# Half-size feature block last, bank copies first, re-ordered loads and setup in a two-layer encoder kernel

## The chip, the cores and the metric

The kernel runs on one core of one Trainium2 chip, as one program. The metric is the device time in microseconds (us); each time is a median of several runs. A profile of one execution is read beside it: PE is TensorE's matmul row and PEld its weight loads, DVE is VectorE, ACT is ScalarE, POOL is GpSimd, SP is SyncE, which issues most of the loads.

## What is computed

Two encoder layers on x (512 tokens by 1024, float32). Each layer adds half of a SwiGLU feed-forward, then three attention mixers that run on the same normalised x, then half of a second feed-forward:

```python
for l in range(DEPTH):                      # 2
    x = x + 0.5 * swiglu(rms_norm(x, ffn1_norm[l]), ffn1_wg[l], ffn1_wu[l], ffn1_wd[l])
    h = rms_norm(x, mix_norm[l])
    ...                                     # h @ w_in[l], split; differential, dilated and latent attention
    x = x + mix @ w_o[l]
    x = x + 0.5 * swiglu(rms_norm(x, ffn2_norm[l]), ffn2_wg[l], ffn2_wu[l], ffn2_wd[l])
# swiglu(x, wg, wu, wd) = (silu(x @ wg) * (x @ wu)) @ wd, with 2816 features
```

## The kernel before

The program is a chain of stages: feed-forward, mixer, feed-forward, and the same again for the second layer. Four feed-forward stages (`ffn`, L249) hold most of the time. Every float32 product is split into a high and a low part in the fast float32r type and made of three matmuls (`mm3`); a weight tile `raw` is split by ScalarE into `whi` (L63) and by VectorE into `wlo` (L64).

**Blocks.** The 2816 features are 22 tiles of 128, worked through in blocks (`FF_BLOCKS`, L38): one block of 2 tiles, then five of 4. For each block an "up" product makes gate and up together, then a "down" product adds the block's share to x. The order is up(0), up(1), down(0), up(2), down(1) and so on; within an up product, after its first two groups, the previous block's result `hid` is transposed and turned into the operand of its down product (`hidden_operand`, L330).

**Seven products.** Both kinds are done by the class `Seven`: a 2 x 2 block product with seven multiplications in place of eight (a Strassen form). `fetch` (L187) loads five keys of weights, 11, u1, 21, u3 and 22, through SyncE; u1 and u3 are the sums of two weights, and the second addend is added by a DMA on GpSimd's queue (L193). For a block of 4 an up product has ten tiles of 512 KB, a down product five; a block of 2 has tiles of half the size. The tiles share ten slots (`N_RAW`). `run` (L225) issues the multiplications into the PSUM banks A, B and D, two banks (t = 0, 1) of each. Where one partial sum belongs to two results, `seed` (L201) copies it, negated, from one bank into another (ScalarE, L208), and TensorE goes on adding there. `done` reads a finished bank: in an up product ScalarE and VectorE write `hid` (L285 to L307), in a down product VectorE adds the bank to x (L316). In a down product the multiplication into A that follows the seed of A is the last one.

**Stage head.** A feed-forward stage transposes x on TensorE (L133), and ScalarE and VectorE make four operands with all their sums (L66, L67, L365 to L368, L168 to L173) in two buffers `c`. `token_factor` (L136) squares x on ScalarE (L141). The mixer (L469) begins in the same way: eight transposes, splits into `xg` (L482), then projections (`project`, L502), which walk the eight k tiles in order.

**Setup.** `setup` (L410) loads gains, bias table, lambdas and the rotary tables. It is emitted after the first feed-forward stage, its DMAs go on GpSimd's queue, and it borrows two weight slots (`oh`, `vec`). Ten `drep` writes broadcast the bias table to DRAM.

**What sets the order.** SyncE's queue is kept as written (`manual_schedule`). The instructions of the other engines are ordered by a planner before the run, by readiness and by the order in which they were emitted; on the chip each engine then works through its own list in order. Two engines that touch the same PSUM bank are put one after the other, in the order of emission, also when both only read.

Of the kernel before, what the change touches and what calls it, by code (L numbers as in the profile page):

```python
# [23 lines left out]
KD = D // P  # L24
# [12 lines left out]

FF_BLOCKS = (2, 4, 4, 4, 4, 4)  # L38


@with_exitstack
def encoder_kernel(ctx: ExitStack, tc, T: dict, out):
# [132 lines left out]
    class Seven:  # L175
# [10 lines left out]

        def fetch(self):  # L187

            for key, ij, plus in (("11", "11", 0), ("u1", "12", "11"), ("21", "21", 0), ("u3", "12", "22"), ("22", "22", 0)):
                for h in range(len(self.parts)):  # L190
                    t = self.raw[key, h] = wload(self.src(ij, h), [P, len(self.parts[h]), self.w])
                    if plus:
                        nc.gpsimd.dma_start(t, self.src(plus, h), accum_op=ALU.add)  # L193
# [31 lines left out]
        def run(self, done):  # L225

            for t, o in self.multiply(I_A11, "11", "A", True, False):
                done("q1", t, o)
                self.seed("B", t, o)
# [8 lines left out]
            self.add("21", "u1", "21")  # L238
            for t, o in self.multiply(I_S3, "u3", "B", False, True):
                done("w", t, o)  # L240
                self.seed("A", t, o)
            last = [lambda: self.multiply(I_S4, "22", "D", False, True), lambda: self.multiply(I_A22, "21", "A", False, True)]
# [5 lines left out]

    def ffn(l, pre, fp, last=False, first=False):  # L249
        def tmp(shape=(P, 512)):  # L250
# [93 lines left out]
        blocks, m0 = [], 0  # L344
# [4 lines left out]

        xa = [operand() for _ in range(4)]  # L350
        if first:
            load_x(0)
        ups = [gate_up(*b) for b in blocks]
        if first:
            ups[0].fetch()
            load_x(1)
        for k in range(4):
            h, lo = xa[k]
# [19 lines left out]

        def run_up(i, between):
            if not (first and i == 0):  # L380
                ups[i].fetch()
            hids[i] = fp.tile([P, NT, 512], F32, tag="c8", bufs=2, name=nm("hid"))
            w = blocks[i][1] * P
            for _ in ups[i].run(gate_up_done(w, hids[i])):
                between()
# [83 lines left out]
    def mixer(l, sb):  # L469
# [11 lines left out]

        xg = []  # L482
        for k in range(KD):
            px = x_transposed(k, "ABCDABDE"[k])
            hl = tuple(t2k("xg", N_XG, F32R) for _ in range(2))
            split(*hl, px, gcol("mix_norm", l, k))
            xg.append(hl)
        r = token_factor(lambda: t2k("a", N_A))
# [13 lines left out]
        def project(c0, n, put, tags="AA"):  # L502

            wl_ = []

            def load():
                cs = c0 if isinstance(c0, tuple) else (c0,)
                w = n // len(cs)
                most = 4 if n <= 256 else 3
                for a in range(0, KD, most):  # L510
                    m = min(most, KD - a)
                    raw = wraw([P, m, n])
                    for i, c in enumerate(cs):
                        nc.sync.dma_start(raw[:, :, i * w:(i + 1) * w], win[:, a:a + m, c:c + w])
                    h, lo = wsplit(raw, [P, m, n])
                    wl_.extend((h[:, k, :], lo[:, k, :]) for k in range(m))

            def piece(t):
                if t == 0:
                    load()  # L520
                pp = bank(tags[t % 2])
                tk = slice(t * P, (t + 1) * P)
                mm3(pp[:, :n], [(a[:, tk], b[:, tk]) for a, b in xg], wl_)
                put(t, pp[:, :n], r[:, t:t + 1])
# [225 lines left out]
        ups = {}  # L750
# [286 lines left out]
    for l in range(L):  # L1037
        with tc.tile_pool(name=f"f{l}", bufs=1, reuse_waits="tile") as fp:
            ffn(l, "ffn1", fp, first=(l == 0))
            if l == 0:  # L1040
                setup()
        with tc.tile_pool(name=f"m{l}", bufs=1, reuse_waits="tile") as mp:
# [52 lines left out]
```

## Time and profile before

| | us |
|---|---|
| median of 3 runs | 2097.91 |
| lowest, highest | 2093.67, 2100.19 |
| the profiled execution | 2097.39 |
| its span, from the first to the last instruction | 2095.6 |

The profile has one row per instruction and engine. A group's busy time is the union of its instructions; "idle before" is the time in which the engine stood still just before them, with the instruction or DMA that released it. Matmul ends are modelled, so a busy TensorE is not TensorE at its peak; the distance from one matmul's start to the next is a safer measure.

### The profile page before, as it was taken

The page shows a single profiled execution, that of the slowest core. Times are in us where ns is not written, and L with a number is a line of the kernel's source. Part 1 is how long each engine was busy: PE and PEld are TensorE (multiplying, and loading weights), DVE is VectorE, ACT ScalarE, POOL GpSimd, SP SyncE. Part 2 cuts the span into 40 slices and gives each one's busy share as a digit, 9 for nine tenths or more (in the row PEclk, how much of TensorE's full clock was granted, in tenths as well). Part 3 has the DMA queues.
Part 4 walks back from the last instruction along what each step waited for, and adds up shares of the span by engine and source line. Part 5 has one row for each costly group of instructions (what it writes and reads, how often), then busy time and mean ns, then how long its engine had stood idle before and what let it go on. Part 6 is the DMA issues. An engine that isn't in the chain of part 4 may idle for free.

```text
span 2095.6 us, 29488 instructions
## 1 busy us (share of the span) xinstructions
PE 1957.7 (93%) x10703; PEld 1674.4 (80%) x10703; DVE 1664.9 (79%) x2485; ACT 1305.5 (62%) x2119; POOL 497.1 (24%) x546
## 2 busy tenths in 40 slices
PE   5999999899989899999989999999998998999998
PEld 5877777799878778777777877779996887778776
DVE  5888888478787688888878888894878867878888
ACT  6655656477876655565566565555778747655654
POOL 3101012244574010101111101002456721111010
PEclk9999999999999999999999999999999999999999
DMA  7777666621212477766567766743212135776671
GB/s 209 195 177 190 176 175 151 177 59 55 63 60 59 121 191 180 186 179 174 126 162 183 177 173 184 183 105 89 71 41 74 56 75 136 191 201 169 172 188 54
DMA packets 181346, 292.79 MB, mean 140 GB/s; under 512 B 13839, under 2 KB 62021, under 8 KB 181200
## 3 DMA queue, kind: packets, MB, share of 16 engines
q1 hardware_dynamic: 137920, 206.74, 31.1%
q0 software_dynamic: 40400, 74.99, 20.9%
q10 hardware_dynamic: 2880, 9.18, 1.4%
q8 instruction: 84, 1.38, 0.3%
q14 instruction: 62, 0.51, 0.1%
HBM read 288.72 MB, written 7.38 MB: 141 GB/s over the span
## 4 chain that ended last, share of the span: by engine, by line
PE 81%; DVE 10%; ACT 5%; issue 2%; DMA 1%; SPq 0%; ACTq 0%; POOL 0%; DVEq 0%; POOLq 0%
PE psA L76 13%; PE psA L78 12%; PE psA L77 12%; PE psB L77 6%; PE psB L76 6%; PE psB L78 6%; PE psD L78 5%; PE psD L76 5%; PE psD L77 5%; DVE wlo L64 2%; PE psD L935 2%; PE psE L964 2%; DVE x L316 2%; PE psE L955 1%; ACT whi L63 1%
## 5 line engine op out<-in xcount | busy, mean ns | idle before, releaser
L64 DVE TENSOR_TENSOR wlo<-raw,whi 128x1024 fp32r<-128x1024 f32 (+2 forms) x566 | 639.1, 1136 | 202.4 <-ACT whi L63 196.5
L63 ACT ACTIVATE whi<-raw 128x1024 fp32r<-128x1024 f32 (+2 forms) x566 | 553.5, 985 | 365.0 <-PE psB L78 127.0
L76 PE MATMUL psA<-whi,s 128*128 128x512 f32 (+1 forms) x840 | 323.9, 390 | 56.2 <-ACT psA L208 37.8
L78 PE MATMUL psA<-whi,s 128*128 128x512 f32 (+1 forms) x840 | 320.5, 383 | 4.1 <-DVE s L263 4.1
L77 PE MATMUL psA<-wlo,s 128*128 128x512 f32 (+1 forms) x840 | 321.0, 382 | 0.0
L76 PEld LDWEIGHTS psA<-whi,s 128*128 128x128 f32 x840 | 161.5, 193 | 99.1 <-ACT psA L208 45.8
L76 PE MATMUL psA<-whi,xg 128*128 128x256 f32 (+3 forms) x752 | 225.5, 301 | 15.7 <-DVE raw L67 4.1
L77 PE MATMUL psA<-wlo,xg 128*128 128x256 f32 (+3 forms) x752 | 220.4, 293 | 0.1
L78 PE MATMUL psA<-whi,xg 128*128 128x256 f32 (+3 forms) x752 | 219.9, 293 | 0.0
L76 PE MATMUL psD<-whi,s 128*128 128x512 f32 (+1 forms) x560 | 203.8, 384 | 14.3 <-ACT s L367 7.8
L77 PE MATMUL psB<-wlo,s 128*128 128x512 f32 (+1 forms) x560 | 214.1, 383 | 1.9 <-DVE wlo L64 1.9
L76 PE MATMUL psB<-whi,s 128*128 128x512 f32 (+1 forms) x560 | 210.0, 388 | 5.8 <-ACT hid L300 3.0
L77 PE MATMUL psD<-wlo,s 128*128 128x512 f32 (+1 forms) x560 | 214.0, 385 | 0.3 <-DVE wlo L64 0.3
L78 PE MATMUL psB<-whi,s 128*128 128x512 f32 (+1 forms) x560 | 211.7, 379 | 0.0
L78 PE MATMUL psD<-whi,s 128*128 128x512 f32 (+1 forms) x560 | 210.4, 381 | 0.6 <-DVE s L368 0.6
L78 PEld LDWEIGHTS psA<-whi,s 128*128 128x128 f32 x840 | 160.7, 192 | 35.7 <-DVE s L263 5.8
L77 PEld LDWEIGHTS psA<-wlo,s 128*128 128x128 f32 x840 | 162.1, 193 | 28.2
L193 POOL DMA_DIRECT2D raw<-in_ffn_wd_dram x48 | 55.2, 1150 | 541.1 <-DMA raw<-in_ffn_wd_dram 367.3
L76 PEld LDWEIGHTS psA<-whi,xg 128*128 128x128 f32 x752 | 144.0, 192 | 24.5 <-DVE raw L67 5.0
L199 DVE TENSOR_TENSOR raw<-raw,raw 128x1024 f32<-128x1024 f32 (+1 forms) x144 | 159.5, 1129 | 0.5
L77 PEld LDWEIGHTS psA<-wlo,xg 128*128 128x128 f32 x752 | 144.3, 192 | 3.2 <-DVE wlo L64 1.0
L78 PEld LDWEIGHTS psA<-whi,xg 128*128 128x128 f32 x752 | 143.8, 191 | 1.4
(241 smaller groups left out, 3849.1 us busy)
## 6 DMA issues: line engine op xcount, KB each, us to landing
raw<-in_ffn_wu_dram SPq DMA_DIRECT2D x120, 512.0 KB, 4.7
raw<-in_ffn_wd_dram SPq DMA_DIRECT2D x100, 512.0 KB, 4.7
raw<-in_ffn_wg_dram SPq DMA_DIRECT2D x80, 512.0 KB, 6.0
raw<-in_ffn_wg_dram POOLq DMA_DIRECT2D x40, 512.0 KB, 8.5
raw<-in_ffn_wu_dram POOLq DMA_DIRECT2D x40, 512.0 KB, 8.7
raw<-in_ffn_wd_dram POOLq DMA_DIRECT2D x40, 512.0 KB, 7.9
raw<-in_w_in_dram SPq DMA_DIRECT2D x40, 256.0 KB, 3.5
toe<-drep ACTq DMA_DIRECT2D x20, 448.0 KB, 3.2
```

The source lines that it names most:

```text
L63: nc.scalar.activation(hi, src, AF.Copy)
L64: eng.tensor_tensor(out=lo, in0=src, in1=hi.bitcast(F32), op=ALU.subtract)
L76: nc.tensor.matmul(o, ah, bh, start=(start and i == 0), stop=False, **kw)
L77: nc.tensor.matmul(o, ah, bl, start=False, stop=False, **kw)
L78: nc.tensor.matmul(o, al, bh, start=False, stop=(stop and i == n - 1), **kw)
L193: nc.gpsimd.dma_start(t, self.src(plus, h), accum_op=ALU.add)
L199: nc.vector.tensor_tensor(out=self.raw[dst, h], in0=self.raw[a, h], in1=self.raw[b, h], op=ALU.add)
L316: nc.vector.scalar_tensor_tensor(out=dst, in0=o, scalar=0.5, in1=dst, op0=ALU.mult, op1=ALU.add)
L935: nc.tensor.transpose(pT[:, kt * P:(kt + 1) * P], e[:, kt * P:(kt + 1) * P], ident)
L955: nc.tensor.matmul(hd.av[:, t * 64:(t + 1) * 64], pt[:, kt * P:(kt + 1) * P], hd.v(kt), start=(kt == 0), stop=(kt == NT - 1),)
L964: nc.tensor.matmul(o, hd.v(kt), x[:, :, kt, :], start=(i + kt == 0), stop=(i == 1 and kt == NT - 1))
```

## The change

Six edits, none of which changes what is computed. The half-size block of a feed-forward stage comes last. In `run` the seed of A is emitted ahead of the other reader of the same bank B, and a `done("q1")` that no reader handles is dropped. The five keys are loaded in the order 11, 21, u1, 22, u3. At the kernel's start only key 11 of the first block is loaded between the two halves of x. `setup` is emitted before the third block's loads in the first stage instead of after the stage. The mixer transposes, splits and multiplies k tiles 4 to 7 (the later half of x) before 0 to 3, and loads its weights in that order.

```diff
--- before.py
+++ after.py
@@ -35,7 +35,7 @@
 V_END, DIL_LATE, LATENT_END, LATENT_V, VALUES_END, OUT_END = 4, 27, 29, 34, 37, 65
 ROOM = 3.5
 
-FF_BLOCKS = (2, 4, 4, 4, 4, 4)
+FF_BLOCKS = (4, 4, 4, 4, 4, 2)
 
 
 @with_exitstack
@@ -184,9 +184,10 @@
         def src(self, ij, h):
             return self.load(int(ij[0]) - 1, int(ij[1]) - 1, self.parts[h])
 
-        def fetch(self):
-
-            for key, ij, plus in (("11", "11", 0), ("u1", "12", "11"), ("21", "21", 0), ("u3", "12", "22"), ("22", "22", 0)):
+        def fetch(self, keys=("11", "21", "u1", "22", "u3")):
+
+            for key in keys:
+                ij, plus = {"u1": ("12", "11"), "u3": ("12", "22")}.get(key, (key, None))
                 for h in range(len(self.parts)):
                     t = self.raw[key, h] = wload(self.src(ij, h), [P, len(self.parts[h]), self.w])
                     if plus:
@@ -225,7 +226,6 @@
         def run(self, done):
 
             for t, o in self.multiply(I_A11, "11", "A", True, False):
-                done("q1", t, o)
                 self.seed("B", t, o)
             for t, o in self.multiply(I_A12, "21", "A", False, True):
                 done("c11", t, o)
@@ -237,8 +237,8 @@
                 done("v", t, o)
             self.add("21", "u1", "21")
             for t, o in self.multiply(I_S3, "u3", "B", False, True):
+                self.seed("A", t, o)
                 done("w", t, o)
-                self.seed("A", t, o)
             last = [lambda: self.multiply(I_S4, "22", "D", False, True), lambda: self.multiply(I_A22, "21", "A", False, True)]
             names = ["q53", "c21"]
             for j in (0, 1) if self.q3_first else (1, 0):
@@ -246,7 +246,7 @@
                     done(names[j], t, o)
 
 
-    def ffn(l, pre, fp, last=False, first=False):
+    def ffn(l, pre, fp, last=False, first=False, aside=lambda: None):
         def tmp(shape=(P, 512)):
             return fp.tile(list(shape), F32, tag="t", bufs=N_T, name=nm("t"))
 
@@ -348,12 +348,12 @@
 
 
         xa = [operand() for _ in range(4)]
+        ups = [gate_up(*b) for b in blocks]
         if first:
             load_x(0)
-        ups = [gate_up(*b) for b in blocks]
-        if first:
-            ups[0].fetch()
+            ups[0].fetch(("11",))
             load_x(1)
+            ups[0].fetch(("21", "u1", "22", "u3"))
         for k in range(4):
             h, lo = xa[k]
             pts = [x_transposed(k + 4 * i, "ABCDABDE"[k + 4 * i]) for i in range(2)]
@@ -377,6 +377,8 @@
         nb = len(blocks)
 
         def run_up(i, between):
+            if i == 2:
+                aside()
             if not (first and i == 0):
                 ups[i].fetch()
             hids[i] = fp.tile([P, NT, 512], F32, tag="c8", bufs=2, name=nm("hid"))
@@ -479,12 +481,13 @@
             return b
 
 
-        xg = []
-        for k in range(KD):
-            px = x_transposed(k, "ABCDABDE"[k])
+        xg = {}
+        ks = [*range(KD // 2, KD), *range(KD // 2)]
+        for i, k in enumerate(ks):
+            px = x_transposed(k, "ABCDABDE"[i])
             hl = tuple(t2k("xg", N_XG, F32R) for _ in range(2))
             split(*hl, px, gcol("mix_norm", l, k))
-            xg.append(hl)
+            xg[k] = hl
         r = token_factor(lambda: t2k("a", N_A))
         cost = {}
         win = T["w_in"][l].rearrange("(k p) c -> p k c", p=P)
@@ -501,26 +504,26 @@
 
         def project(c0, n, put, tags="AA"):
 
-            wl_ = []
+            wl_ = {}
 
             def load():
                 cs = c0 if isinstance(c0, tuple) else (c0,)
                 w = n // len(cs)
                 most = 4 if n <= 256 else 3
-                for a in range(0, KD, most):
+                for a in (4, 0) if most == 4 else range(0, KD, most):
                     m = min(most, KD - a)
                     raw = wraw([P, m, n])
                     for i, c in enumerate(cs):
                         nc.sync.dma_start(raw[:, :, i * w:(i + 1) * w], win[:, a:a + m, c:c + w])
                     h, lo = wsplit(raw, [P, m, n])
-                    wl_.extend((h[:, k, :], lo[:, k, :]) for k in range(m))
+                    wl_.update((a + k, (h[:, k, :], lo[:, k, :])) for k in range(m))
 
             def piece(t):
                 if t == 0:
                     load()
                 pp = bank(tags[t % 2])
                 tk = slice(t * P, (t + 1) * P)
-                mm3(pp[:, :n], [(a[:, tk], b[:, tk]) for a, b in xg], wl_)
+                mm3(pp[:, :n], [(xg[k][0][:, tk], xg[k][1][:, tk]) for k in ks], [wl_[k] for k in ks])
                 put(t, pp[:, :n], r[:, t:t + 1])
 
             fs = [lambda t=t: piece(t) for t in range(NT)]
@@ -1036,9 +1039,10 @@
     gain_columns(16, [big_rows("ffn1_norm")], nc.sync)
     for l in range(L):
         with tc.tile_pool(name=f"f{l}", bufs=1, reuse_waits="tile") as fp:
-            ffn(l, "ffn1", fp, first=(l == 0))
             if l == 0:
-                setup()
+                ffn(l, "ffn1", fp, first=True, aside=setup)
+            else:
+                ffn(l, "ffn1", fp)
         with tc.tile_pool(name=f"m{l}", bufs=1, reuse_waits="tile") as mp:
             mixer(l, mp)
         with tc.tile_pool(name=f"g{l}", bufs=1, reuse_waits="tile") as fp:
```

## Rows read from the trace of the kernel before

**Rows 1.** The page, part 1: TensorE's busy time, share of the span, instructions.

```profile
PE 1957.7 (93%) x10703; PEld 1674.4 (80%) x10703; DVE 1664.9 (79%) x2485; ACT 1305.5 (62%) x2119; POOL 497.1 (24%) x546
```

**Rows 2.** Table by stretch, from:to in us; columns as its first row says.

```profile
core 0: us, PE busy (x) PEld busy (x) DVE busy (x) ACT busy (x) POOL busy (x), PEclk, DMA share, GB/s
0.00:45.00 45.00, 24.18 (x131) 20.59 (x131) 24.26 (x46) 28.41 (x54) 19.06 (x35) 0.96 0.69 195
372.00:390.00 18.00, 10.86 (x54) 8.64 (x52) 7.42 (x20) 7.16 (x19) 0.25 (x1) 0.85 0.80 230
695.00:720.00 25.00, 16.41 (x111) 14.95 (x110) 20.80 (x38) 23.23 (x48) 1.03 (x1) 0.91 0.10 27
720.00:1010.00 290.00, 279.60 (x1295) 231.89 (x1295) 236.17 (x263) 172.54 (x216) 37.93 (x32) 0.99 0.74 189
1010.00:1057.00 47.00, 44.68 (x210) 35.44 (x209) 43.53 (x55) 25.96 (x36) 4.82 (x4) 1.00 0.47 111
```

**Rows 3.** List of waits: who waited for whom, total us, times, longest.

```profile
PE psA L76 <- ACT psA L208: 37.8, 16, 4.6
...
ACT psA L208 <- DVE x L316: 23.8, 9, 5.1
```

**Rows 4.** Timeline, end of a full block's down product: start, us, engine, instruction.

```profile
167.01 0.39 PE L77 MATMUL psB<-wlo,s 128*128 128x512 f32 x1
167.23 0.39 PE L78 MATMUL psB<-whi,s 128*128 128x512 f32 x1
167.36 1.28 DVE L316 SCALAR_TENSOR_TENSOR x<-psB,x 128x512 f32<-128x512 f32 x2
167.66 1.06 ACT L63 ACTIVATE whi<-raw 128x1024 fp32r<-128x1024 f32 x1 [1.57 <-PE psB L78]
...
168.62 1.06 ACT L208 ACTIVATE psA<-psB 128x512 f32<-128x512 f32 x2
...
169.25 0.50 PE L76 MATMUL psA<-whi,s 128*128 128x512 f32 x1 [1.63 <-ACT psA L208]
```

**Rows 5.** Timeline, end of the half-size block's down product.

```profile
107.60 1.18 ACT L208 ACTIVATE psA<-psB 128x512 f32<-128x512 f32 x2 [2.81 <-DVE x L316]
...
108.23 0.80 PE L76 MATMUL psA<-whi,s 128*128 128x512 f32 x1 [4.54 <-ACT psA L208]
```

**Rows 6.** Groups by line, VectorE, one cycle of 60.9 us (172.6 to 233.5).

```profile
L64 DVE TENSOR_TENSOR wlo<-raw,whi 128x1024 fp32r<-128x1024 f32 x21 | 25.4, 1219 | 7.7 <-ACT whi L63 7.5
...
L316 DVE SCALAR_TENSOR_TENSOR x<-psB,x 128x512 f32<-128x512 f32 x4 | 2.6, 676 | 0.0
```

**Rows 7.** Groups by line, VectorE, a stage head (697.7 to 722).

```profile
L368 DVE TENSOR_TENSOR s<-c,s 128x1280 fp32r<-128x1280 f32 x4 | 5.9, 1486 | 0.0
L64 DVE TENSOR_TENSOR wlo<-raw,whi 128x512 fp32r<-128x512 f32 x7 | 4.8, 686 | 0.6 <-ACT whi L63 0.6
```

**Rows 8.** Timeline, TensorE, the first product of that stage head.

```profile
702.34 0.58 PE L76 MATMUL psA<-whi,s 128*128 128x256 f32 x1 [3.54 <-ACT c L365]
```

**Rows 9.** Timeline, TensorE, the second half of x arrives at the start.

```profile
17.19 0.48 PE L133 MATMUL psA<-ident,x 128*128 128x128 f32 x1 [7.18 <-DMA x<-in_x_dram]
```

**Rows 10.** Timeline, POOL, VectorE and TensorE, first feed-forward stage to first mixer.

```profile
371.51 0.74 POOL L456 DMA_DIRECT2D gr<-in_mla_kn_dram  x1 [2.57 <-DVE x L316]
...
384.11 0.23 DVE L462 TENSOR_TENSOR rc<-cs,gr 128x64 f32<-128x64 f32 x1 [7.37 <-DMA gr<-in_mla_kn_dram]
...
386.14 0.48 PE L133 MATMUL psA<-ident,x 128*128 128x128 f32 x1 [5.48 <-DVE x L316]
```

**Rows 11.** Timeline, TensorE, first product of the second mixer.

```profile
1422.90 0.58 PE L76 MATMUL psA<-whi,xg 128*128 128x256 f32 x1 [2.77 <-DVE xg L67]
```

**Rows 12.** DMA issues of the page: KB each, median us from issue to landing.

```profile
raw<-in_ffn_wu_dram SPq DMA_DIRECT2D x120, 512.0 KB, 4.7
...
raw<-in_ffn_wg_dram POOLq DMA_DIRECT2D x40, 512.0 KB, 8.5
```

## The prediction, made before the changed kernel ran

> **What bounds the kernel now.** I read the busy shares first. TensorE is busy 93% of the span, so no other engine can be the limit over the whole [rows 1]. The table by stretch then shows where the other 7% lie. Inside a feed-forward stage TensorE is busy 279.6 of 290 us at a granted clock of 0.99. It idles 20.8 of the first 45 us, 8.6 of the 25 us at the head of the stage after the first mixer, 7.1 of the 18 us between the first feed-forward stage and the first mixer, and 2.3 of the 47 us at a feed-forward end [rows 2]. So what can be won is idle time at the seams, plus whatever gap recurs inside the stages.
>
> The list of waits names that gap. TensorE waits 37.8 us in 16 pieces, at most 4.6 each, for ScalarE's L208, which seeds psA with -psB; and ScalarE in turn waits 23.8 us in 9 pieces for VectorE's L316, which adds the same psB to x [rows 3]. One piece in detail: psB is finished at about 167.5, VectorE reads it from 167.36 to 168.64, ScalarE takes a weight split first (167.66) and starts the seeds at 168.62, TensorE begins psA at 169.25 after 1.63 us idle [rows 4]. In the half-size block the same wait is 4.54 us, because the two L316 stand in VectorE's queue behind older work [rows 5]. Four stages with three of the first kind and one of the second make 4 x (3 x 1.63 + 4.54) = 37.7 us, which is the 37.8 of the list.
>
> The sums below are made against the profiled execution's 2097.4 us (span 2095.6, 1.8 outside it); the median of the runs is 2097.9, which I treat as the same number.
>
> **1. Seed ahead of the other reader (run, L240 and L241).** The seed is now emitted before L316, so that ScalarE can read each psB as soon as its own matmuls end. ScalarE is idle for 1.57 us just before 167.66 [rows 4], and the first psB of the pair is complete six matmuls, 6 x 0.227 = 1.4 us, before the second (pitch 167.01 to 167.23, [rows 4]). A seed takes 0.58 us (two in 1.06), so the first ends about 0.6 us before TensorE needs it: the gap should go. What is late next is VectorE: its two L316 on psB now wait for the seeds, and behind them are queued the lo halves (L64) of the next weights and the L316 on psA. Its second L316 moves from 167.96 to about 168.4, some 0.5 us later, of which its own idle time takes up a part. So I count 85% of 37.8, that is -32 us. Bounds: -19 (half given back) and -38. In the gate/up products the copy that moves back is ScalarE's own L303, with a whole psB group behind it as cover: nothing. The removed q1 call reaches no branch: nothing.
>
> **2. Half-size block last.** The number of products is the same. What moves is 84 TensorE products' worth of short groups (168 of 256 columns, 42 of 512) and VectorE's fixed part of them. For the last three pieces of a stage (up half, down full, down half) TensorE needs about 168 x 0.12 + 84 x 0.227 + 42 x 0.227 = 49 us, with 24 transposes about 51.5 (0.12 is an estimate, half the pitch of rows 4). VectorE's 12 updates of x per down block stay at 0.68 each whatever the size, and its splits cost 1.21 us at full and 0.69 at half size [rows 6, 7]: up half 14 x 0.69 + 4 adds + gating, about 15; down full 7 x 1.21 + 2 x 1.2 + 12 x 0.68 + two operands, about 26; down half 7 x 0.69 + 1.4 + 8.2 + one operand, about 18. That is 59, or 56 after the few per cent by which such instructions overlap. VectorE exceeds TensorE by 4.5 us here, where with a full last block it fell short by about as much. Part of it runs ahead, and one operand fewer is turned at the end: I take +2.5 per stage, +10 in all. Bounds 0 and +6 per stage, +24.
>
> **3. Full-size block first, at three stage heads.** The head is an interval in which four operands are prepared by ScalarE and VectorE: the first product starts after 3.54 us idle [rows 8], and the four L368 alone take 5.9 us of VectorE [rows 7]. Before the first product that needs all sums, TensorE has 48 products. They were of 256 columns (48 x 0.12 = 5.8 us) and become 512 (48 x 0.227 = 10.9): 5.1 us more work under the same preparation. The bigger splits (6 of 1.21 in place of 0.69) give 1 us back. I take -4 at three heads, -12. Bounds 0 (VectorE is so full there, 20.8 of 25 us [rows 2], that the preparation stretches) and -15.
>
> **4. First loads.** TensorE waits 7.18 us for the second half of x, until 17.19 [rows 9], because all ten weight loads of block 0 and its adds are issued ahead of it. Now 1 MB of weights stands between the two halves, twice that of one key before, in place of ten loads of 256 KB. Estimated at the 195 GB/s of that stretch [rows 2], 1.5 MB less is about 7 us of transfer, but the key 21 and the adds then come later and are twice as large. I take -5; bounds 0 and -10.
>
> **5. Setup in the third block.** Today the second gr load is issued at 371.51, lands 12.6 us later behind ten broadcast writes, and VectorE stands still for 7.37 us with two L316 behind the instruction that waits; TensorE idles 5.48 us [rows 10]. After the move this seam is free. But the same chain (two gr loads in turn, ten drep writes on POOL's queue) now runs inside the stage, with POOL's adds of weights queued among it, and VectorE can be stopped there in the same way; two of ten weight tiles are lent meanwhile. TensorE follows VectorE within a microsecond or two, so a stall of 7 us there would cost about 6. I take -4; bounds -6 and +6.
>
> **6. Mixer turns the later half first.** TensorE waits 2.77 us at the second mixer for the first split of x [rows 11], since x's first half is finished last by the down product. The second half is complete some groups earlier, so its transposes and splits can be done before, and the first projection begins with them. ScalarE still squares x there. I take -2.5 twice, -5; bounds 0 and -8. The changed order of loads in every block (21 before u1, 22 before u3) agrees with the order of use, nothing.
>
> Sum: -32 + 10 - 12 - 5 - 4 - 5 = -48, so 2097.4 - 48 = 2049 us.
>
> **Rivals.**
> *VectorE paces instead.* Inside a stage it is busy 236 of 290 us [rows 2] and in the down products without a break [rows 4]; if the freed gaps come back as waits for L64, part 1 shrinks to -19, part 2 grows to +16, part 3 to -6, and with parts 4 to 6 at -5: 2097.4 - 14 = 2083. For it: the second L316 does move back. Against: VectorE waits 7.5 us per cycle for ScalarE's hi halves [rows 6], so it has room in the up products.
> *The recurring gap is a lack of banks.* If the 1.63 us were the wait for a free psA, the new order would not touch it: of part 1 about 12 x 1.63 x 0.85 = 17 us stay, 2066. Against it: the releaser of the gap is the seed, and the seed's own is L316 [rows 3, 4]. The Trainium skill (Perfetto Trace Analysis, Identifying Performance Opportunities) says that the same gap repeating on the engine that should be saturated can mean too few buffers for the next tile; by that rule this rival would hold, and the releasers in the trace speak otherwise.
> *The order of emission is not the order of issue.* Only SyncE's queue is kept as written; the others are ordered by a planner, which may leave the seed behind the split of L63 as it stands today [rows 4]. Then part 1 falls to about -14: 2067.
> *Slower: weight tiles run out at the stage end.* Ten tiles serve 15 loads per 60.9 us cycle now, so one lives about 40 us; up half, down full and down half take 20 tiles in 51.5 us, so one lives 26 us, although half of them are filled only halfway. An added key needs a load (4.7 us), its turn on POOL and an add (8.5) [rows 12], 13 us and more. Should POOL's turns stretch that past 26 us, each microsecond beyond is paid at u1 and u3 of two products in four stages: from 4 us beyond, 4 x 2 x 2 x 4 = 64 us are lost and the kernel is at 2113. It decides only when the chain doubles.
>
> **Chances.** Forecast with its own bounds (2025 to 2068) 0.66; VectorE 0.12; banks 0.06; order 0.06; slower 0.05; still better (below 2025, parts 1, 3 and 4 at their far ends) 0.05. The range that leaves out two in ten reaches from 2020 to 2081. A measurement of this kernel tells about 0.3% (6 us) from no change. All cases but the slower one lie below 2091, with a third of the VectorE case's spread reaching into the 0.3%: faster 0.91, same 0.04, slower 0.05.
>
> **What would show it.** Part 1: the wait of psA for L208 falls from 37.8 to under 8 us, and L316 waits for ACT instead. Part 2: L64 and L316 back to back in the last 15 us of each stage, TensorE idle 2 to 4 us there. Part 3: idle time in the heads below 6 us. Part 5: no wait for gr at the seam, and none over 3 us around 90 to 150 us. Part 6: the first projection within 1 us after the last transpose. It would be wrong if VectorE's queue turned out the limit in the down products, or if waits for loads of u1 or u3 appear at the stage ends.

## The result, and the profile after

The changed kernel took 2038.29 us (median of four, 2036.15 to 2044.61) beside 2099.05 us for the kernel before on the same chip: a ratio of 0.972, 95% interval 0.969 to 0.975. That is 61 us less, where 48 less were forecast; the 2038 lie inside the range of 2020 to 2081. The profiled execution took 2039.07 us with a span of 2037.0.

Part 1 of the page, changed kernel, answers [rows 1]; the span less TensorE's busy time is its idle time.

```profile
PE 1949.2 (96%) x10703; PEld 1665.8 (82%) x10703; DVE 1659.0 (81%) x2485; ACT 1309.3 (64%) x2121; POOL 495.8 (24%) x546
```

TensorE idles 2037.0 - 1949.2 = 87.8 us, where it idled 2095.6 - 1957.7 = 137.9: 50.1 of the 58.6 us between the two spans. The other 8.5 us are busy time of the same 10703 instructions, at a mean granted clock of 0.986 instead of 0.982. VectorE's and ScalarE's work is the same as before, within 6 us.

The lists of waits of the changed kernel (waiter, line, whom it waited for; total, times, longest) answer [rows 3]. The seed copy is L209 now, and the added lines shift the later ones by one or more.

```profile
ACT psA L209 <- PE psB L78: 58.7, 85, 2.1
...
DVE x L316 <- ACT psA L209: 4.6, 19, 0.3
```

TensorE's wait of psA for the seed, 37.8 us before, is no longer in its list. ScalarE now waits for the products themselves instead of for VectorE's adds, and VectorE waits for the seeds, at most 0.3 us at a time. The timeline of the end of a full block's down product, changed kernel, answers [rows 4]:

```profile
191.73 0.39 PE L78 MATMUL psB<-whi,s 128*128 128x512 f32 x1
...
192.16 0.58 ACT L209 ACTIVATE psA<-psB 128x512 f32<-128x512 f32 x1 [0.22 <-PE psB L78]
...
193.22 0.68 DVE L316 SCALAR_TENSOR_TENSOR x<-psB,x 128x512 f32<-128x512 f32 x1
193.32 0.39 PE L76 MATMUL psA<-whi,s 128*128 128x512 f32 x1
193.52 0.58 ACT L209 ACTIVATE psA<-psB 128x512 f32<-128x512 f32 x1 [0.78 <-PE psB L78]
...
194.13 0.69 DVE L316 SCALAR_TENSOR_TENSOR x<-psB,x 128x512 f32<-128x512 f32 x1 [0.23 <-ACT psA L209]
```

The first seed ends at 192.74, and TensorE comes to psA at 193.32 without a gap: the 0.6 us of lead that the prediction worked out. The second add of psB waits 0.23 us.

The table by stretch, changed kernel, answers [rows 2]: the start, the head of a stage, the inside of a stage, its last down products, and its end with the next head.

```profile
core 0: us, PE busy (x) PEld busy (x) DVE busy (x) ACT busy (x) POOL busy (x), PEclk, DMA share, GB/s
0.00:45.00 45.00, 29.90 (x114) 22.55 (x115) 28.71 (x43) 30.96 (x51) 16.44 (x33) 0.92 0.84 245
691.00:720.00 29.00, 27.59 (x108) 21.70 (x109) 26.28 (x33) 22.94 (x31) 1.23 (x1) 0.91 0.25 74
720.00:1010.00 290.00, 288.97 (x1392) 241.62 (x1391) 247.23 (x282) 178.12 (x225) 36.68 (x31) 1.00 0.71 181
1015.00:1030.00 15.00, 12.57 (x58) 9.13 (x59) 15.00 (x23) 9.66 (x16) 2.68 (x3) 1.00 0.95 243
990.00:1037.00 47.00, 38.97 (x196) 30.41 (x194) 42.09 (x62) 29.40 (x52) 8.80 (x8) 0.97 0.88 219
```

Inside a stage TensorE now idles 1.0 of 290 us, where it idled 10.4; before, this stretch held the half-size down product too, with a wait of 4.56 us, and now it ends ahead of it. VectorE does 247 us of work there instead of 236, and TensorE does not wait for it. At the start 15.1 of 45 us are idle (20.8 before). What is left stands at the stage's end and head, in the timeline of TensorE around the seam between two feed-forward stages and of the head at 691 (which answers [rows 8]):

```profile
691.15 0.79 PE L76 MATMUL psA<-whi,s 128*128 128x512 f32 x1 [4.40 <-ACT c L365]
...
717.77 0.50 PE L76 MATMUL psB<-whi,s 128*128 128x512 f32 x1 [1.18 <-ACT hid L300]
...
1018.24 0.74 PE L78 MATMUL psA<-whi,s 128*128 128x512 f32 x2 [1.27 <-DVE s L263]
1028.91 0.44 PE L133 MATMUL psB<-ident,x 128*128 128x128 f32 x2 [1.03 <-DVE x L316]
1031.84 0.77 PE L133 MATMUL psA<-ident,x 128*128 128x128 f32 x5 [0.80 <-DVE x L316]
```

### The profile page after: what moved, and what is told of

Same layout as the page of the kernel before. It is cut to its first block, busy times and chain, and to the rows that moved or that the text cites. A ratio compares the mean times of both kernels' runs of the same rounds, so it can differ in the third digit from the quotient of the medians.

```text
span 2037.0 us, 29494 instructions
## 1 busy us (share of the span) xinstructions
PE 1949.2 (96%) x10703; PEld 1665.8 (82%) x10703; DVE 1659.0 (81%) x2485; ACT 1309.3 (64%) x2121; POOL 495.8 (24%) x546
## 4 chain that ended last, share of the span: by engine, by line
PE 77%; DVE 10%; ACT 5%; DMA 4%; issue 3%; POOL 0%; SPq 0%; DVEq 0%; ACTq 0%; POOLq 0%
PE psA L76 12%; PE psA L78 11%; PE psA L77 11%; PE psB L77 6%; PE psB L76 6%; PE psB L78 6%; PE psD L77 5%; PE psD L78 5%; PE psD L76 5%; DVE wlo L64 3%; DVE x L316 2%; PE psD L938 2%; DMA raw<-in_ffn_wd_dram 2%; PE psE L967 1%; PE psC L552 1%
## 5 line engine op out<-in xcount | busy, mean ns | idle before, releaser
L64 DVE TENSOR_TENSOR wlo<-raw,whi 128x1024 fp32r<-128x1024 f32 (+2 forms) x566 | 633.1, 1131 | 165.2 <-ACT whi L63 158.5
```

Source lines behind the costliest of these rows:

```text
L64: eng.tensor_tensor(out=lo, in0=src, in1=hi.bitcast(F32), op=ALU.subtract)
```

## The experiments

The kernels ran in three groups, each on another chip; the kernel before ran beside each group and took 2097.8 to 2099.4 us. Idle and busy are TensorE's, from part 1 of each page (idle is span less busy), in us.

| kernel | us | ratio to before, 95% interval | idle | busy |
|---|---|---|---|---|
| before (profile of its own) | 2097.9 | 1 | 137.9 | 1957.7 |
| one_seed: only the seed's place | 2074.1 | 0.986 to 0.989 | 117.3 | 1955.1 |
| one_half: only the block order | 2087.2 | 0.994 to 0.996 | 140.5 | 1944.5 |
| seed_half: both | 2052.1 | 0.976 to 0.979 | 111.0 | 1938.6 |
| changed kernel | 2038.3 | 0.969 to 0.975 | 87.8 | 1949.2 |
| no_seed | 2078.8 | 0.989 to 0.992 | 124.6 | 1951.2 |
| no_half | 2067.6 | 0.983 to 0.986 | 106.6 | 1960.5 |
| half_5th | 2058.9 | 0.980 to 0.983 | 103.5 | 1952.8 |
| no_load | 2040.9 | 0.972 to 0.975 | 100.9 | 1938.1 |
| no_aside | 2044.4 | 0.974 to 0.976 | 97.7 | 1944.3 |
| no_mix | 2034.1 | 0.969 to 0.972 | 86.8 | 1944.3 |
| drep_sp | 2041.7 | 0.972 to 0.975 | 94.0 | 1946.0 |
| best1 | 2020.8 | 0.962 to 0.964 | 82.2 | 1938.3 |
| best2 | 2031.8 | 0.967 to 0.969 | 88.1 | 1942.9 |

The lengths of the six stages in the profiled executions, each from its first transpose of x to that of the next (the last to the end of the span; "ff" is a feed-forward stage), in us:

| kernel | ff 1 | mixer 1 | ff 2 | ff 3 | mixer 2 | ff 4 |
|---|---|---|---|---|---|---|
| before | 368.7 | 318.3 | 360.2 | 361.3 | 311.2 | 375.9 |
| one_half | 380.9 | 320.2 | 357.4 | 351.8 | 308.9 | 365.9 |
| changed kernel | 363.4 | 311.5 | 347.8 | 347.0 | 309.1 | 358.2 |
| no_half | 365.9 | 310.0 | 356.2 | 354.9 | 309.7 | 370.3 |
| no_load | 377.3 | 307.9 | 346.0 | 343.1 | 307.9 | 356.8 |
| no_mix | 363.9 | 308.9 | 347.9 | 344.8 | 307.8 | 357.8 |
| best1 | 359.6 | 307.9 | 345.3 | 343.1 | 307.9 | 356.8 |
| best2 | 361.4 | 310.3 | 347.6 | 344.9 | 307.8 | 359.0 |

**The seed alone, and the change without it.** one_seed is the kernel before with this edit (and without the empty q1 call); no_seed is the changed kernel with it undone.

```diff
 for t, o in self.multiply(I_S3, "u3", "B", False, True):
+    self.seed("A", t, o)
     done("w", t, o)
-    self.seed("A", t, o)
```

> The kernel before with only the seed's place changed: seed(A) ahead of done(w), and the q1 call gone. Theory S (the gap of 1.63 us, and of 4.54 us in the half-size block, is made by VectorE's L316 standing ahead of the seed at the same bank): the whole 37.7 us go, 2097.9 - 37 = about 2061 us, TensorE's wait of psA for the seed is under 3 us, ScalarE's wait for L316 is gone, and L316 waits for ScalarE by under 6 us instead. Theory V (VectorE paces the down products and takes half back): about 2079 us, with new TensorE waits for L64 of some 18 us. Theory P (the planner's order keeps the seed behind the split of L63): about 2084 us, the wait of psA still over 20 us.

> The changed kernel with only the seed's place set back (done(w) ahead of seed(A)). Theory S, if the gain doesn't depend on the other parts: 2038 + 37 = about 2075 us, the wait of psA for the seed is back at 35 to 38 us. Theory V: about 2057 us. If the half-size block at the stage's end makes the same gap dearer than the 4.54 us that it cost at the front (VectorE has more queued there): 2080 us or more.

Alone the edit took 25 us off, inside the changed kernel it is worth 40. The list of TensorE's waits of one_seed shows where the first falls short of 37:

```profile
PE psA L76 <- DVE x L315: 15.3, 4, 3.8
...
PE psA L76 <- ACT psA L208: 1.8, 3, 0.6
```

The twelve gaps of 1.63 us in the full blocks are gone (19.6 us; idle time fell by 20.6). The four in the half-size blocks, 4.54 us each in [rows 5], are still 3.8 us each, but VectorE ends them now and not the seed. Its timeline in one_seed at that place, with ScalarE's seeds and TensorE's restart:

```profile
103.21 1.28 ACT L208 ACTIVATE psA<-psB 128x512 f32<-128x512 f32 x2
...
105.11 0.40 PE L78 MATMUL psA<-whi,s 128*128 128x512 f32 x1
109.34 0.80 PE L76 MATMUL psA<-whi,s 128*128 128x512 f32 x1 [3.84 <-DVE x L315]
```

```profile
106.48 0.68 DVE L315 SCALAR_TENSOR_TENSOR x<-psD,x 128x512 f32<-128x512 f32 x1
107.08 0.68 DVE L315 SCALAR_TENSOR_TENSOR x<-psB,x 128x512 f32<-128x512 f32 x1
107.68 0.41 DVE L173 TENSOR_TENSOR c<-c 128x256 f32<-128x256 f32 x1
108.01 0.68 DVE L315 SCALAR_TENSOR_TENSOR x<-psB,x 128x512 f32<-128x512 f32 x1
108.61 0.68 DVE L315 SCALAR_TENSOR_TENSOR x<-psA,x 128x512 f32<-128x512 f32 x1
```

The seeds are done at 104.5; VectorE works on without a break, adds five results to x among the other work, and only when the first psA is added (109.29) does TensorE get a bank for the next product. So Theory S holds for the full blocks. In the half-size ones VectorE sets the pace, as in Theory V, though TensorE waits for a bank that VectorE has not added yet and not for L64. Theory P falls: the seeds came early enough in the full blocks, but for three new waits of 0.6 us in the last one of a stage. In no_seed, where the half-size block is last, the seed's wait is 26.2 us in 19 pieces, not 35 to 38, and another 9.8 us are a wait for the operands of the last block (four of up to 2.5 us, where the changed kernel waits 1.1 to 1.3). The size was right, its place only in part.

**The place of the half-size block.** one_half is the kernel before with the second line, no_half and half_5th are the changed kernel with the first and the third, and seed_half is the kernel before with the second line and the seed's edit.

```diff
-FF_BLOCKS = (2, 4, 4, 4, 4, 4)
+FF_BLOCKS = (4, 4, 4, 4, 4, 2)
# half_5th:
+FF_BLOCKS = (4, 4, 4, 4, 2, 4)
```

> The kernel before with only FF_BLOCKS = (4, 4, 4, 4, 4, 2). Theory H1 (the prediction's sum: the tails lose 2.5 us each, +10, three heads win 4 us each, -12): -2, about 2096 us. Theory H2 (read from the stage times of the changed kernel: three feed-forward stages are 14.5 to 18.6 us shorter, of which the seed accounts for 9.4, so that the place of the half-size block would win 5 to 9 us in each): about -20, 2078 us. Theory H3 (the heads win nothing and the tails lose as in the far bound): +15, 2113 us.

> The changed kernel with only FF_BLOCKS = (2, 4, 4, 4, 4, 4), the half-size block first again. Theory H1 (heads and tails cancel): 2038 + 2 = about 2040 us. Theory H2 (5 to 9 us in each of three or four stages): about 2058 us, the idle time in the heads of the stages back, and the tails little changed. Theory H3: about 2023 us.

> The changed kernel with the half-size block fifth of six: FF_BLOCKS = (4, 4, 4, 4, 2, 4). A full block is first in every stage, as in the changed kernel, and the last is full, as in the kernel before. Theory T1 (what costs is the half-size down product itself: inside a stage its adds of x make TensorE wait 3.8 us for psA, and some 3 us more go at the half clock that follows): that wait is back in four stages, at the fifth block, 4 x 3.8 to 4 x 6.8, so 2053 to 2065 us. Theory T2 (the gain of the new order is made in the heads, by the full block first): the heads stay as short, no such wait, 2038 us within 5. The prediction's sum, by which the half block at the end costs 2.5 us in each tail: about 2028 us.

> The kernel before with two edits together: the seed's new place and FF_BLOCKS = (4, 4, 4, 4, 4, 2). Alone they took 25 and 12 us off. Theory I (they need each other: in the half-size block at the front the seed alone leaves a wait of 3.8 us for the adds of x, four times, with a half clock behind it; and the half-size block alone leaves the seed's wait in all five full blocks): -25 - 12 - 15 = -52, about 2047 us. Theory N (they are independent, and the rest of the 61 us comes from the other parts): -37, about 2062 us.

Inside the changed kernel the block order is worth 29 us (no_half), beside the seed alone 21.5 (seed_half less one_seed), and by itself 12 (one_half). H3 falls; no_half lies beyond H2, and one_half midway between H1 and H2. By itself the order also makes the start dearer: ten loads of a full block now stand ahead of the second half of x, TensorE's longest wait for x is 21.9 us in one_half in place of the 7.18 of [rows 9], and the first stage is 12.2 us longer than before. Where the 29 come from: the table by stretch of no_half, and then of the changed kernel, in the same stage around the half-size down product.

```profile
core 0: us, PE busy (x) PEld busy (x) DVE busy (x) ACT busy (x) POOL busy (x), PEclk, DMA share, GB/s
772.00:774.00 2.00, 2.00 (x9) 1.16 (x7) 2.00 (x4) 1.88 (x3) 0.00 (x0) 1.00 0.93 329
774.00:778.00 4.00, 0.27 (x2) 0.00 (x0) 4.00 (x8) 2.34 (x3) 2.20 (x2) 0.87 0.71 174
778.00:782.00 4.00, 3.91 (x9) 3.13 (x10) 4.00 (x7) 0.96 (x2) 0.21 (x1) 0.50 1.06 239
782.00:784.00 2.00, 2.00 (x6) 1.52 (x6) 2.00 (x2) 1.75 (x2) 0.00 (x0) 0.55 1.13 213
784.00:786.00 2.00, 2.00 (x10) 1.61 (x10) 1.45 (x1) 1.04 (x2) 0.00 (x0) 1.00 0.17 29
```

```profile
770.00:790.00 20.00, 20.00 (x97) 16.58 (x97) 19.34 (x26) 10.14 (x13) 2.88 (x3) 1.00 0.75 187
```

VectorE is busy through all of 772 to 784; TensorE idles 3.82 us, and when it goes on, its granted clock is at 0.50 (the 1.2 GHz level) for four microseconds and at 0.55 for two more, in which 15 products run. At the pitch of 0.227 us that the full clock gives they would take 3.4 us, so 2.6 are lost on top: 6.4 us in this stage, and 26 in four if all were like it. That is an estimate: the four feed-forward stages of no_half are 2.5, 8.4, 7.9 and 12.1 us longer, with heads and tails in them. The heads give a part: TensorE's idle pieces there are 3.54, 1.75, 0.64, 1.88 and 0.76 in no_half (8.6 us) and 4.40, 0.78 to 1.18 and some small ones in the changed kernel (under 6), while the tail lost about 1 us.

half_5th came out at 2058.9, inside what T1 gave, and the heads, which it shares with the changed kernel, can't be the cause (T2 falls, and so does the sum of the prediction by which the last place is the dear one). But T1's mechanism was only half right. Its list of TensorE's waits:

```profile
PE psA L76 <- ACT s L262: 17.7, 4, 4.4
...
PE psA L76 <- DVE x L316: 5.7, 9, 1.7
```

The wait for the adds is small (0.8 us in each stage); instead the operands of the last, full block come 4.4 us late, four times. VectorE makes their sums in the same unbroken run of adds (344.1 to 353.9 in the first stage). So the half-size down product overloads VectorE wherever it stands, and something behind it in VectorE's queue is late: the next product's bank when it is first, the next block's operands when it is fifth. At the end nothing follows but the transposes of x, and these wait 1.0 and 0.8 us.

seed_half gives 46.9 us, where the two alone sum to 25.4 + 12.2 = 37.6: they do need each other, by 9 us, not by the 15 that Theory I gave.

**The first loads and the order of the keys.** no_load is the changed kernel with both undone; best1 (below) keeps the first loads and undoes the order of the keys and that of the mixer.

```diff
-def fetch(self, keys=("11", "21", "u1", "22", "u3")):
+def fetch(self, keys=("11", "u1", "21", "u3", "22")):
...
-ups[0].fetch(("11",))
+ups[0].fetch()
 load_x(1)
-ups[0].fetch(("21", "u1", "22", "u3"))
```

> The changed kernel with the first loads and the order of the keys set back (all ten weight loads of block 0 between the two halves of x; 11, u1, 21, u3, 22). Theory L1 (the prediction's -5 for this part): about 2043 us. Theory L2 (the part is worth far more beside a full-size first block, since its ten loads are 512 KB each: with the half-size block alone moved to the end, TensorE waited 21.9 us for the second half of x, in place of 7.2): 12 to 16 us, about 2052 us, with a wait for x of some 20 us at the start.

The wait for x at the start grew as L2 says, yet the run is only 2.6 us above the changed kernel. The timeline of no_load's start, which answers [rows 9]:

```profile
30.55 0.47 PE L133 MATMUL psA<-ident,x 128*128 128x128 f32 x1 [21.25 <-DMA x<-in_x_dram]
```

In the changed kernel this wait is 2.55 us. The 19 us that it loses are nearly made up by everything else: idle time is 13.1 us more, not 19, and busy time is 11.1 us less, at a mean granted clock of 0.992 instead of 0.986. So another part of this edit had to cost something, and the order of the keys was the candidate. That was tried next.

**best1 and best2.** best1 is the changed kernel with these edits; best2 adds a sum by VectorE for the first block.

```diff
-def fetch(self, keys=("11", "21", "u1", "22", "u3")):
+def fetch(self, keys=("11", "u1", "21", "u3", "22")):
...
-ups[0].fetch(("21", "u1", "22", "u3"))
+ups[0].fetch(("u1", "21", "u3", "22"))
...
-ks = [*range(KD // 2, KD), *range(KD // 2)]
+ks = [*range(KD)]
-for a in (4, 0) if most == 4 else range(0, KD, most):
+for a in range(0, KD, most):
# best2, besides: u1 of block 0 is loaded without the adding transfer, and
+self.add("u1", "u1", "11")   # ahead of the product that uses it
```

> The changed kernel with the second half of x still loaded ahead of all weights but the key 11, but the keys in the old order (11, u1, 21, u3, 22) and the mixer in the order 0 to 7. Theory K (the order of the keys cost something: u1 needs a load and an add and now comes later, so that TensorE waits 4.7 us for it at the start; the wait for x stays at 2.6 us): about 2028 us, the 4.7 us gone. Theory Z (the differences of the runs without one part are of the half clock, not of the order): 2034 to 2038 us.

> The kernel of the run before it in this group (old order of keys behind the second half of x, mixer 0 to 7), and the sum u1 of the very first block made by VectorE from two loaded tiles, in place of GpSimd's adding transfer: 1 MB less to load at the start, for two adds of 1.2 us. Theory K2 (the start is bound by the loads): 2 to 4 us less than that kernel. Theory V2 (VectorE, which prepares the operands at the start, is later by its two adds): 0 to 3 us more than it.

best1 is the fastest of all, 2020.8 us, 17.5 below the changed kernel and with an interval that lies clear of its own. Against no_load, with the same keys, it is 17.7 us shorter in the first stage and at most 0.7 in any later one: that is what the first loads are worth, and the mixer's order is worth nothing here. Against no_mix, from which only the keys tell it apart, it is 13.3 us faster (0.962 to 0.964 against 0.969 to 0.972): the kernel with the order that agrees with the order of use is 13 us slower. A part can be read. In GpSimd's timeline of the changed kernel, where the setup runs:

```profile
113.90 1.22 POOL L194 DMA_DIRECT2D raw<-in_ffn_wg_dram  x1
115.71 3.66 POOL L436 DMA_DIRECT2D drep<-dvec  x7 [0.59 <-DMA dvec<-vec]
...
129.13 1.26 POOL L194 DMA_DIRECT2D raw<-in_ffn_wg_dram  x1 [2.81 <-ACT whi L63]
```

and in best1:

```profile
105.51 1.23 POOL L194 DMA_DIRECT2D raw<-in_ffn_wg_dram  x1
111.47 1.21 POOL L194 DMA_DIRECT2D raw<-in_ffn_wg_dram  x1 [4.72 <-DVE rs L467]
...
117.81 4.14 POOL L436 DMA_DIRECT2D drep<-dvec  x8 [2.48 <-DMA dvec<-vec]
```

With u1 loaded second, both its adds stand ahead of the ten broadcast writes; with u1 third, the second add stood behind them, 15 us later than the first. Not all 15 are the writes': the last of them ended at 126.33, and GpSimd then waited for ScalarE; and SyncE's load of that half had stood 6.9 us until dvec had landed. ScalarE's split waited until the add landed at 147.3, 18 us after its issue (the page's median for these adds is 6.2), and TensorE behind it; the second line is not in best1:

```profile
147.33 1.06 ACT L63 ACTIVATE whi<-raw 128x1024 fp32r<-128x1024 f32 x1 [6.55 <-DMA raw<-in_ffn_wg_dram]
148.44 0.50 PE L76 MATMUL psD<-whi,s 128*128 128x512 f32 x1 [2.95 <-ACT whi L63]
```

That is 3 us of the 13. Between the spans of no_mix and best1 (10.6 us), 4.6 are idle time and 6.0 are busy time of the same instructions, at a mean granted clock of 0.992 instead of 0.989. The clock does not explain the 13 us, though: the two fastest executions of best1 (2020.5 and 2020.6 us) and of no_mix (2032.9 both) all ran at 0.989. K's own mechanism, the wait for u1 at the start, failed: it is 4.14 us in best1 and 4.67 in the changed kernel. What the other 10 us are is open. The planner's order differs between the two kernels in every stage, and best2 shows that an edit at the start alone moves the later stages by 8.6 us in all.

best2 is 11 us slower than best1, where 3 were the most that V2 gave. At the start VectorE's two adds put later operands back (a wait of 4.10 us at 43.33, ended by ScalarE's L370); but most of the loss lies in stages whose code is the same: the first mixer is 310.3 us in place of 307.9, and the feed-forward stages behind it are 1.8 to 2.3 us longer. There the planner had set the order anew. That this is the cause is not shown: the second mixer is re-ordered too, and takes 307.8 us beside 307.9.

**The setup in the third block.** no_aside moves it back behind the stage; drep_sp leaves it and issues the ten writes from SyncE.

```diff
# no_aside
-ffn(l, "ffn1", fp, first=True, aside=setup)
+ffn(l, "ffn1", fp, first=True)
+setup()
# drep_sp
-nc.gpsimd.dma_start(drep[h], dvec[h:h + 1, :].to_broadcast([P, 1024]))
+nc.sync.dma_start(drep[h], dvec[h:h + 1, :].to_broadcast([P, 1024]))
```

> The changed kernel with the setup emitted after the first feed-forward stage again. Theory A1 (the prediction's -4): about 2042 us. Theory A2 (the seam is dearer beside the half-size block at the end: 15 us of gaps there in the run with that block alone moved, against 3.6 us in the changed kernel, less the 4.6 us that the setup costs inside the stage now): about 2045 us. Theory A3 (what the seam wins is lost inside the stage): 2038 us within 2.

> The changed kernel with the ten broadcast writes of the setup issued by SyncE in place of GpSimd. Theory D1 (the writes in GpSimd's queue hold back its adds of weights, which costs TensorE 1.7 and 2.9 us at 132 and 148 us): both waits go, about 2034 us. Theory D2 (SyncE then waits for dvec to land, and the weight loads behind it come late): new waits for loads around 120 to 140 us, 2038 us or more.

no_aside is 6.1 us slower, between A1 and A2, in intervals that just overlap; A3 falls. Its timeline at the seam, TensorE, answers [rows 10]:

```profile
375.40 0.58 PE L76 MATMUL psA<-whi,xg 128*128 128x256 f32 x1 [10.62 <-DVE xg L67]
381.35 0.58 PE L78 MATMUL psA<-whi,xg 128*128 128x256 f32 x1 [4.51 <-DVE xg L67]
```

15 us of idle time beside 3.6 in the changed kernel. Inside the stage the move costs the 2.95 us shown above and this wait of the changed kernel, which best1 has too; no_aside has neither:

```profile
131.60 0.50 PE L76 MATMUL psA<-whi,s 128*128 128x512 f32 x1 [1.69 <-DVE x L316]
```

drep_sp is 3.4 us slower, in intervals that overlap. D1's 2034 did not come, and the waits are those of D2. The list of SyncE's waits from 95 to 140, and TensorE's timeline:

```profile
SPq L436 <- DMA dvec<-vec: 28.5, 1, 28.5
SPq L152 <- DMA drep<-dvec: 10.0, 8, 2.2
```

```profile
137.50 0.80 PE L76 MATMUL psA<-whi,s 128*128 128x512 f32 x1 [9.15 <-ACT whi L63]
```

SyncE stood 28.5 us in front of the first write until dvec had landed, with the weight loads behind it; GpSimd's next adds, which D1 wanted earlier, began only at 142.44. The Trainium skill (DMA: Bandwidth & Descriptors, Issuing engines are not separate DMA queues) says that all issuing engines feed the same transfer engines, so that another issuer saves only issue time. The runs agree that nothing was won, and show what was lost: the place in the queue.

**The mixer's order.** no_mix undoes it (the two lines `ks` and `for a` above).

> The changed kernel with the mixer's transposes, splits and first projections in the order 0 to 7 again. Theory M1 (the prediction's 2.5 us at each of two mixers): about 2043 us, the first projection waiting 3 us or more for a split. Theory M2 (x's two halves are finished almost together, so the order matters little): 2038 to 2040 us.

4 us faster without the part, in intervals that overlap (0.969 to 0.972 and 0.969 to 0.975): no gain, and no cost that is told for certain. The first products of the first mixer, TensorE's timeline of the changed kernel, answer [rows 11]:

```profile
373.47 0.39 PE L76 MATMUL psA<-whi,xg 128*128 128x256 f32 x1 [0.98 <-DVE xg L67]
...
375.71 0.58 PE L76 MATMUL psA<-whi,xg 128*128 128x256 f32 x1 [1.62 <-ACT xg L66]
```

and of no_mix:

```profile
375.82 0.39 PE L76 MATMUL psA<-whi,xg 128*128 128x256 f32 x1 [2.76 <-DVE xg L67]
```

One wait of 2.76 us has become two of 0.98 + 1.62 = 2.60, and the same holds in the second mixer, which [rows 11] shows. M1 falls. The stages between the mixers, whose instructions stand in the same order in both runs, differ by up to 2.2 us, so that much can be told from nothing.

## Why the prediction was right, and where its steps were not

**What bounds it** was read rightly: 50 of the 58.6 us came out of TensorE's idle time, most of it at the places named; the rest is busy time at a higher mean clock. That VectorE would pace instead (2083) did not come, except in the half-size block. The rival by which the gap is a lack of banks (2066) falls for the full blocks: the pool of banks is as it was, and the 1.63 us are gone in one_seed. In the half-size block the 3.8 us that the seed left are such a wait, for a psA that VectorE had not added yet. The Trainium skill's reading of a repeated bubble (Perfetto Trace Analysis, Identifying Performance Opportunities) is worded as a possibility; here the releaser decided. The order of emission did become the order of issue. No wait for u1 or u3 appeared at the stage's end, so the slower case did not come.

**1. The seed (-32).** The mechanism is shown; the step that failed is the 85% laid over all sixteen pieces. The twelve of 1.63 us went entirely, with the lead of 0.6 us that was worked out; the four of 4.54 us in the half-size block kept 3.8 us each under another name. The prediction had seen that two L316 stand there "behind older work", and priced the piece as if the seed alone were what held it. Alone the term measures -25, beside the other parts -40.

**2 and 3. The half-size block (+10 and -12).** This is the part that was sized worst: -2 predicted, -12 alone, -21.5 beside the seed and -29 beside all other parts. That VectorE has the more work in the last pieces fits the rows: from 1015 to 1030 it is busy 15.00 of 15 us, and TensorE 12.57. What was left out is that the same excess stood at the front before, and was paid there with a gap and the half clock behind it, 6.4 us in the stage that was read; the step compared the tail with that of a full block and did not credit the front. The tail's own cost, waits of 1.27, 1.03 and 0.80 us where 1.15 and 1.02 stood before, is some 1 us, within its bounds. The head's gain of 4 us was about 3. Nor did the sum say that the order by itself makes the wait for x at the start 14.7 us longer, which part 4 then has to take away.

Parts 1 to 3 together: -34 predicted, -47 measured (seed_half). The rest, -14 predicted, measured 2052.1 - 2038.3 = 13.8, but by terms that offset each other:

**4. First loads (-5).** The stretch up to 45 us idles 15.1 in place of 20.8 us, 5.7 less, which agrees with the -5 by luck. The edit by itself is worth about 18 us (no_load and best1: 100.9 and 82.2 us of idle time, the same busy time), since with a full block first the ten loads ahead of x are twice as large: 21.25 us of wait in place of 7.18 in [rows 9]. The step that failed is that the loads taken away were counted at the half-size block's 256 KB. The order of the keys, "nothing" in the prediction, cost 13 us. The step that failed there is the argument from the order of use: u1 is used after 21 but needs a transfer more, on a queue that others block, and its lead was not counted. This accounts for 3 of the 13 us.

**5. Setup (-4).** Measured -6. No wait for gr at the seam, as expected; the waits for gr on VectorE are 1.76 and 1.01 us. The warning that GpSimd's adds would queue among the broadcast writes came true with 2.95 us of TensorE's time, less than the 6 feared; the other wait inside the stage, 1.69 us, was for VectorE.

**6. Mixer (-5).** Measured nothing. The first wait fell below 1 us as said, but the step looked at the first product alone: the next one waits for the first half of x, and the sum stayed at 2.6 us.

So the forecast was near in part by luck: the block order and the first loads were both undervalued, and an unseen cost of 13 us offset that.

## What to carry to other kernels

When two engines read one bank, put first the reader whose result TensorE waits for; here the other lost at most 0.3 us at a time. Place the piece in which the second engine has more work than TensorE where nothing queued behind it is needed soon, and price such a gap with the half clock that follows it. When ordering loads, count extra transfers and the queue that they stand in, and not the order of use alone; and check a part that "costs nothing" by undoing it alone. Where a planner orders the rest, expect shifts of some 2 us in stages that were not edited.

## What the runs showed of the hardware

- A gap of 3.82 us on TensorE was followed by six microseconds at a granted clock of 0.50 to 0.55, and 15 products in them took 2.6 us longer (no_half, from 774 us), two thirds of the gap on top of it.
- The same 10703 TensorE instructions were busy 1938.1 us in one kernel and 1960.5 in another, a spread of 22 us at mean granted clocks of 0.992 and 0.979 (no_load, no_half). That is as much as several parts of the change are worth, and it does not go by the amount of idle time, which is 100.9 and 106.6 us. The mean clock, which also counts idle time, gives busy time only roughly: seed_half is busy 1938.6 us at 0.987.
- Ten broadcast writes on GpSimd's queue, begun once an earlier write had landed, stood from 115.7 to 126.3 us in front of its next add of weights; issued from SyncE, they held its loads 28.5 us until that write had landed.
